# Three loads instead of one ahead of the barrier on entry, in a softmax kernel that is bound by its transfers

## The chip, the cores and the metric

The kernel runs on one core of one Trainium2 chip. The metric is the device time of one execution in microseconds (us); medians of several runs are given. A profile of one execution goes with each kernel. The engines that matter here: VectorE (DVE in the profile), ScalarE (ACT), GpSimd (POOL), SyncE (SP, which issues the loads), and the 16 DMA engines that carry out all loads and stores.

## The reference

```python
x = np.random.randn(16, 1024, 512).astype(np.float32)      # 33.55 MB in, 33.55 MB out

def reference(x):
    x_max = np.max(x, axis=-1, keepdims=True)
    exp_x = np.exp(x - x_max)
    return (exp_x / np.sum(exp_x, axis=-1, keepdims=True)).astype(np.float32)
```

## The kernel before

The 16,384 rows are cut into ten chunks; R is the number of rows that each of the 128 partitions gets. The first chunks are small, so that work can start early. All chunks live in one buffer of SBUF (the on-chip memory) of 96 rows per partition; the last two use places that earlier chunks have left.

```python
CHUNKS = [
    (3, 0), (5, 3), (8, 8), (16, 16), (16, 32), (16, 48), (16, 64), (16, 80), (16, 0), (16, 16),
]                                        # (rows R, place in SBUF)
...
EARLY = 8                                # loads issued at the start
AFTER_STORE = {2: [8], 3: [9]}
GROUP = 8
...
STORE_ROWS = {3: 8, 4: 8, 5: 8}          # chunks not named here are stored whole
ON_ACT = ()                              # loads issued by ScalarE instead of SP
AT_HEAD = {mybir.EngineType.SP: 1}
```

The program begins with a barrier of all engines (line 164 in the profiles). This function takes the first loads of SP out of the body and puts them ahead of SP's part of that barrier:

```python
def loads_at_the_head(nc):
    main, body = nc.main_func.blocks[0], nc.main_func.blocks[1]
    for engine, count in AT_HEAD.items():
        loads = [ ... the engine's first `count` DMA copies in body ... ]
        barrier = ... the engine's first InstDrain in main ...
        for load in loads:
            body.instructions.remove(load)
        main.instructions[barrier:barrier] = loads
```

The schedule, shortened:

```python
    for k, (R, _) in enumerate(CHUNKS):
        m = max(1, round(R / GROUP))     # groups of about 8 rows
        ...
    for k in range(EARLY):
        load(k)                          # nc.sync.dma_start
    for g, (k, a, _, _) in enumerate(groups):
        ...
        rowmax(g)     # VectorE, line 101: reduce_max, negated
        exps(g)       # ScalarE, line 109: exp with bias, and the row's sum
        scale(...)    # VectorE, lines 121, 123: reciprocal, multiply; then the store, issued by ScalarE, line 129
```

## Time and profile before

| | before |
|---|---|
| time, median of the 3 first runs | 161.57 us (161.53 to 161.69) |
| span of the profiled execution | 159.7 us |
| VectorE busy | 123.9 us (78%) |
| ScalarE busy | 93.3 us (58%) |
| bytes moved | 67.1 MB, mean 420 GB/s |

VectorE is at 78% over the span, but at 98% from 60 to 140 us, and idle at both ends.

### The profile page before, as it was taken

How to read it: one execution, taken by the hardware profiler on the slowest of the kernel's cores; microseconds unless marked ns; L12 is line 12 of the kernel's file. 1: busy time of each engine (PE TensorE's matmuls, PEld its weight loads, DVE VectorE, ACT ScalarE, POOL GpSimd, SP SyncE). 2: the span in 40 equal slices, each digit the busy share in tenths (PEclk: the TensorE clock that was granted, in tenths of full speed). 3: DMA queues.
4: the chain of work that ended last, by engine and by line, in shares of the span. 5: the costliest groups of instructions: out<-in, count | busy, mean ns of one | idle time of the engine just before them, and what ended most of it. 6: DMA issues, size and time to landing. Idle time of an engine off the chain costs nothing.

```text
span 159.7 us, 521 instructions
## 1 busy us (share of the span) xinstructions
DVE 123.9 (78%) x162; ACT 93.3 (58%) x257; POOL 0.2 (0%) x4
## 2 busy tenths in 40 slices
DVE  0481870799699999999999999999999999762000
ACT  0718129208994959595868677686859595930000
POOL 0000000000000000000000000000000000000000
DMA  7999999899999999999999999999999999999993
GB/s 269 433 464 411 389 447 446 383 412 466 402 441 431 460 435 396 439 418 468 427 414 439 414 484 427 396 447 402 435 439 476 418 402 468 443 402 468 427 410 164
DMA packets 3315, 67.13 MB, mean 420 GB/s; under 512 B 368, under 2 KB 368, under 8 KB 624
## 3 DMA queue, kind: packets, MB, share of 16 engines
q1 hardware_dynamic: 1440, 33.56, 49.5%
q10 hardware_dynamic: 1872, 33.56, 48.9%
q14 instruction: 3, 0.02, 0.0%
HBM read 33.55 MB, written 33.55 MB: 420 GB/s over the span
## 4 chain that ended last, share of the span: by engine, by line
DVE 70%; ACT 14%; issue 3%; DMA 3%; DVEq 0%; ACTq 0%
DVE shift L101 38%; DVE held L123 30%; ACT held L109 14%; DMA held<-in_x_dram 3%; DVE recip L121 2%; DVEq L175 0%; ACTq L109 0%
## 5 line engine op out<-in xcount | busy, mean ns | idle before, releaser
L109 ACT ACTIVATE held<-held,shift 128x512 f32<-128x512 f32 x128 | 90.5, 709 | 43.4 <-DVE shift L101 33.2
L101 DVE TENSOR_REDUCE shift<-held 128x8 f32<-128x4096 f32 (+2 forms) x17 | 70.6, 4161 | 4.5 <-DMA held<-in_x_dram 4.5
L123 DVE TENSOR_SCALAR held<-held,recip 128x512 f32<-128x512 f32 x128 | 52.2, 481 | 0.6
L109 ACT ACTIVATION_READ_ACCUMULATOR held<-held,shift 128x1 f32 x128 | 24.0, 187 | 0.0
L121 DVE RECIPROCAL recip<-sums 128x8 f32<-128x8 f32 (+2 forms) x17 | 3.3, 193 | 15.8 <-ACT held L109 15.8
L109 ACT ACT_TABLE_LOAD x1 | 1.3, 1283 | 4.5 <-DMA held<-in_x_dram 4.5
L164 POOL MEMSET const-bfloat16-1.0<- 128x1 bf16 x1 | 0.1, 102 | 0.0
L164 POOL MEMSET const-uint8-127<- 128x1 uint8 x1 | 0.1, 102 | 0.0
L164 POOL MEMSET const-float32-1.0<- 128x1 f32 x1 | 0.1, 99 | 0.0
L164 POOL MEMSET const-float32-0.0<- 128x1 f32 x1 | 0.1, 98 | 0.2 <-issue 0.2
## 6 DMA issues: line engine op xcount, KB each, us to landing
held<-in_x_dram SPq DMA_DIRECT2D x7, 4096.0 KB, 41.8
out_dram<-held ACTq DMA_DIRECT2D x4, 4096.0 KB, 21.0
out_dram<-held ACTq DMA_DIRECT2D x7, 2048.0 KB, 35.5
held<-in_x_dram SPq DMA_DIRECT2D x1, 2048.0 KB, 11.3
held<-in_x_dram SPq DMA_DIRECT2D x1, 1280.0 KB, 6.7
out_dram<-held ACTq DMA_DIRECT2D x1, 1280.0 KB, 20.0
held<-in_x_dram SPq DMA_DIRECT2D x1, 768.0 KB, 4.5
out_dram<-held ACTq DMA_DIRECT2D x1, 768.0 KB, 15.7
```

The costliest lines, as they stand in the source:

```text
L101: nc.vector.reduce_max(out=shift[g], in_=place[k][:, a:b, :], axis=AX, negate=True)
L109: nc.scalar.activation(out=place[k][:, r, :], in_=place[k][:, r, :], func=EXP, bias=shift[g][:, r - a : r - a + 1], scale=1.0, accum_out=s ...
L121: nc.vector.reciprocal(out=recip, in_=sums[g])
L123: nc.vector.tensor_scalar_mul(out=place[k][:, r, :], in0=place[k][:, r, :], scalar1=recip[:, r - a : r - a + 1],)
L164: nc = _bacc.Bacc("TRN2", target_bir_lowering=False, num_devices=1)
```

## The change

The intent: when the first load's bytes are through, the next loads should already stand in the queue. Two lines change.

```diff
-AT_HEAD = {mybir.EngineType.SP: 1}
+AT_HEAD = {mybir.EngineType.SP: 3}
...
-        m = max(1, round(R / GROUP))
+        m = -(-R // GROUP)
```

## The prediction

> **What bounds the kernel now.** I read the page's picture of the 40 slices first, to see which resource is full and where it isn't.
>
> ```profile
> DVE  0481870799699999999999999999999999762000
> ACT  0718129208994959595868677686859595930000
> DMA  7999999899999999999999999999999999999993
> GB/s 269 433 464 411 389 447 446 383 412 466 402 441 431 460 435 396 439 418 468 427 414 439 414 484 427 396 447 402 435 439 476 418 402 468 443 402 468 427 410 164
> ```
>
> A slice is 159.7 / 40 = 4.0 us. The DMA row is full everywhere but in the first and the last slice. VectorE (DVE) is full in the middle but idle in the last three or four slices, while the DMA engines still work. So the bytes set the end: 33.55 MB in and 33.55 MB out. To see how full "full" is, and what happens in the first microseconds, I asked for busy time in chosen windows; the last three columns are granted clock, DMA share and GB/s.
>
> ```profile
> 0.00:1.00 1.00, 0.00 (x0) 0.00 (x0) 0.20 (x4) 1.00 0.00 0
> 1.00:2.00 1.00, 0.00 (x0) 0.00 (x0) 0.00 (x0) 1.00 0.98 289
> 2.00:3.00 1.00, 0.00 (x0) 0.00 (x0) 0.00 (x0) 1.00 0.94 362
> 3.00:4.00 1.00, 0.00 (x0) 0.00 (x0) 0.00 (x0) 1.00 1.07 432
> 8.00:60.00 52.00, 40.27 (x49) 28.84 (x81) 0.00 (x0) 1.00 1.01 429
> 60.00:140.00 80.00, 78.41 (x104) 60.21 (x169) 0.00 (x0) 1.00 1.00 432
> 140.00:157.00 17.00, 3.46 (x9) 1.21 (x4) 0.00 (x0) 1.00 1.00 432
> ```
>
> At 432 GB/s the 67.1 MB alone need 155.3 us of the 159.7. Only 4.4 us of the span are anything else. At the head: 1.0 us with no byte moved, then two microseconds below the later rate, which lose (432 - 289) / 432 + (432 - 362) / 432 = 0.33 + 0.16 = 0.5 us. The other 2.9 us are the tail and the small shortfalls between. The change can only touch the head, so this 1.5 us (0.9% of the time) is all that it could ever win.
>
> Next, when SP issues its loads (columns: start, duration, engine and line; I put four narrow windows of the timeline under each other), and when the barrier on entry comes.
>
> ```profile
> 0.00 0.37 SPq L96 DMA_DIRECT2D held<-in_x_dram  x1
> ...
> 0.78 0.33 SPq L96 DMA_DIRECT2D held<-in_x_dram  x1
> ...
> 1.16 0.42 SPq L96 DMA_DIRECT2D held<-in_x_dram  x1
> ...
> 1.63 0.59 SPq L96 DMA_DIRECT2D held<-in_x_dram  x1
> ```
>
> ```profile
> L164 SPq DRAIN  x1: 131/131/131, 0.4 to 0.4; - x1
> L164 SPq EVENT_SEMAPHORE  x1: 17/17/17, 0.7 to 0.7; - x1
> ```
>
> The first load is issued at 0.00, then SP drains, goes through the barrier at 0.7, and issues the second load at 0.78, the third at 1.16, the fourth at 1.63. Between the end of the first issue (0.37) and the start of the second (0.78) lie 0.41 us, where two issues that follow each other in the body are only some 0.05 us apart (0.78 + 0.33 = 1.11 to 1.16). So the barrier costs SP about 0.36 us.
>
> Last, who uses these loads, and when (timeline of VectorE and of ScalarE's last store; then the page's issues with the time to landing in the last column):
>
> ```profile
> 4.48 1.75 DVE L101 TENSOR_REDUCE shift<-held 128x3 f32<-128x1536 f32 x1 [4.48 <-DMA held<-in_x_dram]
> ...
> 9.93 2.81 DVE L101 TENSOR_REDUCE shift<-held 128x5 f32<-128x2560 f32 x1
> ...
> 18.65 4.41 DVE L101 TENSOR_REDUCE shift<-held 128x8 f32<-128x4096 f32 x1
> ...
> 144.77 0.34 ACTq L129 DMA_DIRECT2D out_dram<-held  x1
> ```
>
> ```profile
> held<-in_x_dram SPq DMA_DIRECT2D x1, 2048.0 KB, 11.3
> held<-in_x_dram SPq DMA_DIRECT2D x1, 1280.0 KB, 6.7
> ...
> held<-in_x_dram SPq DMA_DIRECT2D x1, 768.0 KB, 4.5
> ```
>
> The first load lands at 4.46 and releases VectorE. The second lands at 0.78 + 6.7 = 7.5 and is read at 9.93, with 2.4 us to spare; the third lands at 1.16 + 11.3 = 12.5 and is read at 18.65, with 6.2 us to spare. Neither of the two loads that move is waited for. The chain of waits goes through VectorE, but its last instruction releases a 2 MB store at 144.77, which alone would need 2.1 MB / 432 GB/s = 4.9 us and so could be over by 150; the DMA runs to 158.5 (last packet in the trace) because earlier stores stand before it. VectorE therefore has some 8 us in hand at the end.
>
> **What the Trainium skill says.** Four places of the page "DMA: Bandwidth & Descriptors" bear on this. (1) "Queues, rings and completion order": on each DMA engine a queue's descriptors are consumed in ring order. The trace agrees: the packet records of the second load (10,240 bytes each) begin at 3.12 us, as those of the first (6,144 bytes) run out on one engine after another, though it was issued at 0.78. (2) "Latency and other measured facts": the first byte of a transfer issued by SP or ScalarE comes after about 600 ns. Here the first packet starts at 1.02 us, 0.65 us after the end of its issue (0.37). (3) "Specifications": a ceiling of 435 GB/s for the 16 engines; the trace moves 432 GB/s from 60 to 157 us, so there is no faster state for the change to reach. (4) "Issuing engines are not separate DMA queues": starting transfers concurrently on several engines saves only the sequencer's issue time. The change also saves issue time only, though on one engine; what that is worth is worked out below.
>
> **The change part by part.** *The grouping line.* m = max(1, round(R / 8)) becomes the ceiling of R / 8. For the sizes used, 3, 5, 8 and 16, the old line gives 1, 1, 1, 2 and the new one 1, 1, 1, 2. The order of instructions agrees: VectorE's 52 rows, ScalarE's 29 and the others are identical, and only SP's order differs. Cost: 0.
>
> *The loads at the head.* Nothing is removed or added. Two DMA issues of SP move from behind the barrier to before it. First the second load: its issue would begin at 0.37 + 0.05 = 0.42 instead of 0.78, the third at 0.42 + 0.33 + 0.05 = 0.80 instead of 1.16, each 0.36 us earlier. For that to be worth something, an engine must have run dry before the second load came. With the 1.02 us from start of issue to first packet, the second load was ready to move at 0.78 + 1.02 = 1.80, and the first engine became free for it at 3.12. It stood in the queue for 1.3 us already; now it stands there from 1.44, for 1.7 us. Gain on the path: 0.
>
> *The barrier.* SP arrives at it after three issues instead of one: 0.80 + 0.42 = 1.22 instead of 0.37, so 0.85 us later, and the others pass it at about 0.7 + 0.85 = 1.55. VectorE and ScalarE have nothing to do until the first load lands at 4.46, so 2.9 us of slack remain. ScalarE's table load also began only after that landing, at 4.53, and lay beside the first reduction. Loss on the path: 0.
>
> *The fourth load on.* SP's sum up to the fourth issue is the same three issues and one barrier in another order, so it still starts near 1.6, and its packets begin only at 11.25 us in the trace. The sixth load waits for the first one's landing (4.47) and the two last wait for stores; none of these moves. Effect: 0.
>
> Sum: 0 gained at the head, 0 lost, DMA bytes and rate unchanged. Predicted time: the time before, 161.6 us rounded.
>
> **The rivals.** *An idle DMA is filled, so it is faster.* For it: the first slice shows 269 GB/s and there is a 0.41 us hole in SP. Against it: in the windows 1:2 and 2:3 the engines are 98% and 94% busy already; the rate is low because the packets take long (the first ones 0.3 to 0.7 us, later ones of the same size 0.23 us), not because none are queued. If earlier queueing did lift these two microseconds to the full rate, 0.5 us would go: 161.1. The first 1.0 us stays, as the first load's issue doesn't move.
>
> *The first load now shares the engines with the next two, and lands late.* If the three were served in turn and not in ring order, the first would land after some 3 x 0.79 = 2.4 MB instead of 0.79 MB: 1.6 MB / 432 GB/s = 3.7 us later. VectorE would end near 148.4, still before the stores are through, and the DMA would have loads to move meanwhile. The time would grow by a few tenths, at most about 1 us: 161.6 to 162.6. Ring order in the trace speaks against it.
>
> *The later barrier becomes the wait.* It would need to pass 4.46, 3.8 us later than before, where two issues cost 0.85. If it did by x us, VectorE's 8 us in hand would take it up first. Time: 161.6.
>
> *The order of loads and stores falls differently.* Any shift of a tenth of a microsecond may change how packets of the two queues alternate. The slices vary from 383 to 484 GB/s, but even out over windows of 50 us and more (429, 432). I allow 0.3 us either way for it.
>
> **Range and chances.** The three runs before lie within 0.16 us (161.53 to 161.69). Beside this come the 0.3 us of the last rival, 0.5 us at best from a better start, and at worst about half a microsecond of a late first load. I take 161.55, with 161.0 to 162.1. Faster by over 2% would need 3.2 us, twice the whole 1.5 us at the head: 0.01. Slower by over 2% would need a stall that no view suggests: 0.01. Within 2%: 0.98.
>
> **What would show each step right or wrong.** In the profile after: SP issues at about 0.00, 0.42 and 0.80, the fourth near 1.6; the barrier at about 1.55. The first reduction still starts at 4.4 to 4.6; if it starts past 5, the sharing rival holds. The window from 1 to 4 us keeps about 360 GB/s (289, 362 and 432 before); if it rises above 400, the idle-DMA rival holds. The second load's issue to landing grows by about 0.36, from 6.7 to 7.1, as it waits longer in the queue and lands at the same 7.5; the third's from 11.3 to 11.7. The window from 60 to 140 us stays at 430 GB/s. The prediction is wrong if the span leaves 159.1 to 160.3, or if the mean rate in the middle moves by more than 1%.

## The result, and the profile after

| | before | after |
|---|---|---|
| time, median (range) of 4 runs | 161.56 (161.53 to 161.69) | 161.61 us (161.46 to 161.69) |
| ratio, with its 95% interval | | 1.0001 (0.9983 to 1.0018) |
| span of the profiled execution | 159.7 | 159.7 us |

Ratios here and below are the mean time of one kernel's fast runs over that of the other's of the same rounds, so they are not quite the ratio of the medians quoted. The outputs are correct. The time is the same.

The picture of the 40 slices after:

```profile
DVE  0481870799699999999999999999999999762000
ACT  0718029208994959595867777686859594930000
DMA  7999999899999999999999999999999999999993
GB/s 274 436 464 424 389 425 464 375 404 466 410 445 443 456 415 412 439 415 480 419 415 427 410 501 410 412 435 402 447 439 476 402 419 484 402 419 460 427 410 164
```

The DMA row is the same digit for digit, the first slice included. The chosen windows after (granted clock, DMA share and GB/s are the last three columns):

```profile
0.00:1.00 1.00, 0.00 (x0) 0.00 (x0) 0.20 (x4) 1.00 0.00 0
1.00:2.00 1.00, 0.00 (x0) 0.00 (x0) 0.00 (x0) 1.00 0.98 264
2.00:3.00 1.00, 0.00 (x0) 0.00 (x0) 0.00 (x0) 1.00 0.93 387
3.00:4.00 1.00, 0.00 (x0) 0.00 (x0) 0.00 (x0) 1.00 1.09 442
60.00:140.00 80.00, 78.36 (x104) 60.18 (x169) 0.00 (x0) 1.00 1.00 432
```

The first microsecond still moves nothing, the next three move 264 + 387 + 442 = 1093 KB against 289 + 362 + 432 = 1083 KB before, and the middle runs at the same 432 GB/s. SP's issues (four narrow windows of the timeline) and its part of the barrier (the line's own view) after:

```profile
0.00 0.37 SPq L96 DMA_DIRECT2D held<-in_x_dram  x1
...
0.42 0.42 SPq L96 DMA_DIRECT2D held<-in_x_dram  x1
...
0.89 0.43 SPq L96 DMA_DIRECT2D held<-in_x_dram  x1
...
1.73 0.51 SPq L96 DMA_DIRECT2D held<-in_x_dram  x1
```

```profile
L164 SPq DRAIN  x1: 125/125/125, 1.4 to 1.4; - x1
L164 SPq EVENT_SEMAPHORE  x1: 17/17/17, 1.6 to 1.6; - x1
```

So the edit did what it was meant to do: the second load is issued 0.36 us earlier, the third 0.27 us, and the barrier falls 0.9 us later. Its users, and the last store, after (timeline), and the three issues with the time to landing in the last column:

```profile
4.40 1.75 DVE L101 TENSOR_REDUCE shift<-held 128x3 f32<-128x1536 f32 x1 [4.40 <-DMA held<-in_x_dram]
...
9.85 2.81 DVE L101 TENSOR_REDUCE shift<-held 128x5 f32<-128x2560 f32 x1
...
144.71 0.34 ACTq L129 DMA_DIRECT2D out_dram<-held  x1
```

```profile
held<-in_x_dram SPq DMA_DIRECT2D x1, 2048.0 KB, 11.4
held<-in_x_dram SPq DMA_DIRECT2D x1, 1280.0 KB, 7.0
...
held<-in_x_dram SPq DMA_DIRECT2D x1, 768.0 KB, 4.4
```

The second load now takes 7.0 us to land where it took 6.7, and so lands at 0.42 + 7.0 = 7.4 us against 7.5. Almost all of what SP gained is spent waiting in the queue. The first load lands at 4.4 us as before, and VectorE starts with it.

### The profile page after: what moved, and what is told of

Its sections match the earlier page's. It is cut to its first block, busy times and chain, and to the rows that moved or that the text cites. A ratio compares the mean times of both kernels' runs of the same rounds, so it can differ in the third digit from the quotient of the medians.

```text
span 159.7 us, 521 instructions
## 1 busy us (share of the span) xinstructions
DVE 123.9 (78%) x162; ACT 93.3 (58%) x257; POOL 0.2 (0%) x4
## 4 chain that ended last, share of the span: by engine, by line
DVE 71%; ACT 14%; issue 3%; DMA 3%; DVEq 0%; ACTq 0%
DVE shift L101 38%; DVE held L123 30%; ACT held L109 14%; DMA held<-in_x_dram 3%; DVE recip L121 2%; DVEq L175 0%; ACTq L109 0%
```

## The experiments

The main theory: the DMA engines have work from the first packet to the last, so only the moment of the first packet and the bytes count; a load that is queued before it is needed gains nothing by being queued earlier. Rivals: VectorE's chain sets the end; SP's hole between the loads costs time; several loads at once hurt the first. All runs below give correct outputs unless it is said.

A yardstick serves for several of them: the bytes moved in the first 8 us, from the windows view. A deficit divided by 432 GB/s is what the end should lose if the transfers set it. The kernel before moves 8 x 350 = 2800 KB, the changed one 8 x 354 = 2832 KB.

**No load at the head.**

```diff
-AT_HEAD = {mybir.EngineType.SP: 1}
+AT_HEAD = {}
```

> No load is ahead of the barrier; all ten follow it. Main theory (the DMA engines are full from the first packet to the end, so only the issue of the first load counts, and how many follow it at the head does not): the first issue moves from before the barrier to behind it, some 0.6 to 0.7 us later on the clock of the other engines, so the time grows by about 0.6 us to 162.2 us (162.0 to 162.4). Rival (VectorE's chain or the middle sets the end and has several us in hand): no change, 161.6 us. A rate in the middle of 432 GB/s in either case.

Measured: 162.32 us (162.26 to 162.50), ratio 1.0036 (1.0019 to 1.0054). The first load is issued at 0.73 us, and 8 x 322 = 2576 KB are moved in 8 us: a deficit of 224 KB, or 0.5 us. The mean of the runs grew by 0.0036 x 161.6 = 0.6 us. So moving the *first* load does pay, most of its 0.73 us (0.3 to 0.9 us by the interval); the head of the program is on the path.

**Five loads at the head.**

```diff
-AT_HEAD = {mybir.EngineType.SP: 3}
+AT_HEAD = {mybir.EngineType.SP: 5}
```

> Five loads ahead of the barrier. SP reaches it after five issues, and the others pass it near 2.7 us (0.7 before, 1.65 with three). Main theory: all wait for the first load's landing at 4.4 to 4.5 us anyway, so no change: 161.6 us (161.4 to 161.8). Rival (more issues ahead of the barrier cost or win a little each, and with three they cancelled): a drift of 0.2 us or more away from the kernel before, in either direction.

Measured: 161.61 us (161.54 to 161.83), ratio 0.9992 (0.9975 to 1.0010). SP passes the barrier at 3.1 us instead of 0.7, later than the 2.7 expected because one issue took 0.94 us, and nothing comes of it. One, three and five loads give the same time: only the first of them counts, and the barrier has room up to the first landing.

**Seven and eight loads at the head: the barrier made to be the wait.**

```diff
-AT_HEAD = {mybir.EngineType.SP: 3}
+AT_HEAD = {mybir.EngineType.SP: 7}        # and 8
```

> Seven loads ahead of the barrier; the sixth and seventh wait for the landing of the first and the second load, so SP reaches the barrier near 7.8 us, and VectorE starts near 7.9 instead of 4.4: a shift of 3.4 to 3.5 us of its whole chain. By the prediction on record (8 us in hand at the end): no change, 161.6 us. By the packet records, read again after the result: the last store is 4 MB and not 2 MB, it is issued at 144.77 and its packets begin at 147.65 on the first DMA engine and at 148.85 on the last, so it was ready (issue + 1.02 = 145.8) only 1.9 to 3.0 us early; the shift is then 0.4 to 1.6 us too long: 162.0 to 163.2 us.

> Eight loads ahead of the barrier; the eighth waits for the third load's landing at 12.4 us, so VectorE starts near 12.9 instead of 4.4: a shift of 8.4 us. By the prediction on record (8 us in hand): 162.0 us at most. By the packet records (1.9 to 3.0 us in hand): 5.4 to 6.5 us slower, 167.0 to 168.1 us, if no wait inside VectorE's chain takes up a part.

Measured: with seven 162.38 us (162.35 to 162.51), ratio 1.0033 (1.0015 to 1.0050); with eight 176.89 us (176.79 to 177.03), ratio 1.0930. Timeline of the run with seven:

```profile
8.46 1.75 DVE L101 TENSOR_REDUCE shift<-held 128x3 f32<-128x1536 f32 x1 [8.46 <-PEq L164]
...
148.76 0.34 ACTq L129 DMA_DIRECT2D out_dram<-held  x1
```

And of the run with eight:

```profile
22.75 1.75 DVE L101 TENSOR_REDUCE shift<-held 128x3 f32<-128x1536 f32 x1 [22.75 <-PEq L164]
...
163.04 0.34 ACTq L129 DMA_DIRECT2D out_dram<-held  x1
```

VectorE is now released by line 164, the barrier, and no longer by the load. With seven it starts 8.46 - 4.40 = 4.06 us later than in the changed kernel, and the last store is issued 148.76 - 144.71 = 4.05 us later: nothing inside VectorE's chain takes up the shift. In the packet records no packet is in flight at 149.5 us, and the last store's first 16 packets begin at 149.61 to 149.75 us, so the DMA engines had run out of work, and the last packet ends at 159.51 instead of 158.47. Of 4.05 us, 1.04 reached the end, so VectorE had 3.0 us in hand. With eight the shift is 22.75 - 4.40 = 18.35 us and the last packet ends at 173.78, 15.3 us later: again 3.0 us in hand. (These are differences of single profiled runs; by the ratios, which compare with the kernel before in the same rounds, the losses are 0.5 and 15.0 us, and the room 3.5 and 3.3 us. So it is about 3 us.) My expected shift for eight (8.4 us) was wrong, since the eighth load is issued only at 21.98 us, after the fourth load's landing, and not after the third's at 12.4; the sum of shift and room holds all the same. The 8 us of the prediction are refuted.

**Less work for VectorE.** Wrong result on purpose: only the first row of each group is multiplied.

```diff
-        for r in range(a, b):
+        for r in range(a, a + 1):
             nc.vector.tensor_scalar_mul(
```

> The changed kernel, but only the first row of each group is multiplied by the reciprocal (111 of 128 multiplications gone; the result is wrong on purpose, all loads and stores stay). VectorE loses about 111 x 0.41 = 45 us. Main theory (bytes set the end): no change beyond 0.5 us, 161.1 to 162.0 us, with VectorE idle part of the middle. Rival (VectorE's chain sets the end): tens of us faster, or at least the 1.9 us that its last store would come earlier.

Measured: 161.80 us (161.75 to 161.87), ratio 0.9998 (0.9983 to 1.0013). The page of that run:

```profile
DVE 81.1 (51%) x51; ACT 92.5 (58%) x257; POOL 0.2 (0%) x4
```

VectorE loses 123.9 - 81.1 = 42.8 us of work and the time doesn't move. Together with the two runs before: VectorE does not set the end, but it is only about 3 us of delay away from doing so.

**The first two loads in two queues.** The second load goes to ScalarE's head.

```diff
-ON_ACT = ()
+ON_ACT = (1,)
-AT_HEAD = {mybir.EngineType.SP: 3}
+AT_HEAD = {mybir.EngineType.SP: 1, mybir.EngineType.Activation: 1}
```

> The first load at SP's head and the second at ScalarE's head, both before the barrier, so the two stand in different queues of the same DMA engines. Main theory (within one queue the first load is served first; of two queues the engines take turns): the first load lands later than 4.4 us, between 5.0 and 6.4, and the second earlier than 7.5; VectorE starts 0.6 to 2.0 us later, inside the 1.9 to 3.0 us that it has in hand, so the time stays within 0.3 us of 161.6. If the first load lands at 4.4 to 4.6 here as well, taking turns does not show, and ring order is not what protected it in the changed kernel.

Measured: 161.76 us (161.62 to 161.87), ratio 0.9994 (0.9979 to 1.0010). Issues of that run:

```profile
held<-in_x_dram ACTq DMA_DIRECT2D x1, 1280.0 KB, 9.7
...
held<-in_x_dram SPq DMA_DIRECT2D x1, 768.0 KB, 5.8
```

The first load takes 5.8 us instead of 4.4, and VectorE starts at 5.87. The Trainium skill says why ("DMA: Bandwidth & Descriptors", "Queues, rings and completion order"): an engine takes turns between the queue rows that have work. In the changed kernel the three loads stand in one queue and the first lands at 4.4 us, so it is this order that protects it. The 1.5 us that VectorE loses here are inside its 3.0 us, and the time stays. I had expected the second load to land earlier than 7.5 us; it landed at 0.1 + 9.7 = 9.8, because SP's third load now shared with it (93 of its 128 packets start between 5.0 and 9.8 us).

**The second load held back.** The converse of the change, made from the kernel before: the load must wait until an engine has written to its place.

```diff
         for k in range(EARLY):
+            if k == 1:
+                nc.vector.memset(place[1][:, 0:2, :], 0.0)
             load(k)
```

> The kernel before with the second load held back on purpose until VectorE has cleared 2 rows of its place (about 1 us), so it is issued near 1.4 to 2.0 us and not at 0.78. Main theory: ready to move at issue + 1.02 = 2.4 to 3.0 us, still before the first DMA engine runs out of the first load at 3.1 us, so no change: 161.6 us (161.4 to 161.8), and the window from 1 to 4 us keeps some 360 GB/s. Rival (each tenth of a microsecond of SP's hole between the two loads costs time, so closing it should have paid): 0.6 to 1.2 us slower, 162.2 to 162.8 us.

For the long hold the added line is `nc.vector.tensor_copy(out=place[1][:, 0, 0:1], in_=place[0][:, 0, 0:1])`, which waits for the first load.

> The kernel before with the second load held back until the first has landed and VectorE has copied one element of it: issued at 4.6 to 4.7 us, first packet near 5.7. Main theory: the slowest DMA engine ends its part of the first load near 4.1 us and then stands still until 5.7, so every byte behind it comes 1.5 to 2.0 us later: 163.1 to 163.6 us. Rival (VectorE's chain sets the end, DMA has time in hand): the second load lands near 11.5 instead of 7.5 us, 1.5 us after VectorE wants it at 10.0, and the time grows by 0 if VectorE has more than that in hand.

Measured: short hold 163.24 us (163.01 to 163.32), ratio 1.0090 (1.0072 to 1.0108); long hold 164.54 us (164.52 to 164.66), ratio 1.0174 (1.0152 to 1.0195). The long hold confirms the mechanism and shows that I sized it too small. Its windows:

```profile
3.00:4.00 1.00, 0.00 (x0) 0.00 (x0) 0.00 (x0) 1.00 0.39 160
4.00:5.00 1.00, 0.48 (x2) 0.43 (x1) 0.00 (x0) 1.00 0.00 0
5.00:6.00 1.00, 1.00 (x1) 0.86 (x1) 0.00 (x0) 1.00 1.03 164
```

I had counted the stop of the slowest engine, about 1.6 us from 4.1 to 5.7. But at 3.5 us only 3 packets are in flight, so 13 of the 16 engines stand still by then; the mean over all engines is 2.3 us. In addition, from 5 to 6 us they are busy and move only 164 GB/s: the first 16 packets after the stop take 1.03 us on average and up to 1.40, where the median of that size is 0.385, so they lose another 0.6 us. Together that is 2.9 us. The yardstick has 8 x 190 = 1520 KB, a deficit of 1280 KB or 3.0 us; the mean grew by 2.8 us.

The short hold is a miss: issued at 1.99 us, 1.2 us later than before, it should have cost nothing by the prediction's margin of 1.3 us, and it cost 0.0090 x 161.6 = 1.5 us. In its packet records most DMA engines begin the second load by 4.2 us, but two only at 6.4 and 6.6 us, though the last engine had ended its part of the first load at 4.15. (The records name no engine; what they show is 14 packets in flight instead of 16 until 6.3 us.) The end is uneven too: the 16 engines finish between 157.87 and 160.22 us, two of them after 160, against 157.33 to 158.53 before. That these are the same two is likely and not shown.

**A control, and three more doses.** The control clears two rows at the same time, but in the eighth load's place, so that the second load isn't held:

```diff
+            if k == 7:
+                nc.vector.memset(place[7][:, 0:2, :], 0.0)
```

> Control for the short hold: the same clearing of 2 rows by VectorE at the same moment, but in the place of the eighth load, which is issued late in any case; the second load is not held. If the 1.6 us of the short hold came from holding the second load: no change here, 161.6 us (161.4 to 161.8). If they came from VectorE writing while the first load arrives: 163.0 to 163.3 us again.

The other three are the short hold with one element cleared (`place[1][:, 0, 0:1]`), with one row (`place[1][:, 0, :]`), and with two rows cleared by GpSimd (`nc.gpsimd.memset`).

> The second load held until VectorE has cleared one element of its place: issued near 1.15 us instead of 0.78, so held back by as much as the change brings it forward. If the queue's margin is what the prediction says (1.3 us): no change, 161.6 us (161.4 to 161.8). If the margin is smaller and is used up step by step, so that the short hold's 1.2 us of delay cost 1.6 us: some 0.3 to 0.5 us slower, 161.9 to 162.1 us.

> The second load held until VectorE has cleared one row of its place: issued near 1.5 us instead of 0.78, 0.75 us later than before. By the prediction's margin of 1.3 us: no change, 161.6 us (161.4 to 161.8). If there is a threshold that depends on the last DMA engine to be fed rather than the first, between 1.5 and 2.0 us: no change here either, against 1.6 us at 1.99. If the loss grows in step with the delay: about 1.0 us slower, 162.6 us.

> The short hold again, but GpSimd clears the 2 rows and VectorE does nothing extra: the second load issued between 1.9 and 2.8 us. If holding the load is the cause, whoever holds it: 1.0 to 2.2 us slower, 162.6 to 163.8 us, and some DMA engines begin the second load late again. If VectorE's write was: 161.6 us. It also tells whether two engines standing still until 6.4 us was an accident of one trace or comes back.

Measured, with the other runs in order of the second load's issue:

| run | second load issued at, us | KB in the first 8 us | median (range), us | ratio (95%) |
|---|---|---|---|---|
| changed kernel | 0.42 | 2832 | 161.61 (161.46 to 161.69) | 1.0001 (0.9983 to 1.0018) |
| control, not held | 0.78 | 2816 | 161.61 (161.54 to 161.67) | 0.9992 (0.9972 to 1.0011) |
| one element | 0.92 | 2408 | 162.49 (162.14 to 163.43) | 1.0057 (1.0026 to 1.0087) |
| one row | 1.46 | 2328 | 162.37 (162.20 to 163.16) | 1.0051 (1.0025 to 1.0076) |
| GpSimd, two rows | 1.75 | 2592 | 163.07 (162.63 to 163.74) | 1.0085 (1.0061 to 1.0109) |
| short hold | 1.99 | 2400 | 163.24 (163.01 to 163.32) | 1.0090 (1.0072 to 1.0108) |
| long hold | 4.71 | 1520 | 164.54 (164.52 to 164.66) | 1.0174 (1.0152 to 1.0195) |

The control clears VectorE's write of blame, and GpSimd's version shows that it does not matter who holds the load. The surprise is the smallest dose. Its second issue, and its windows:

```profile
0.92 0.33 SPq L96 DMA_DIRECT2D held<-in_x_dram  x1
```

```profile
3.00:4.00 1.00, 0.00 (x0) 0.00 (x0) 0.00 (x0) 1.00 0.92 334
5.00:6.00 1.00, 1.00 (x1) 0.92 (x1) 0.00 (x0) 1.00 0.93 276
```

And the window from 3 to 4 us of the run with one row:

```profile
3.00:4.00 1.00, 0.00 (x0) 0.00 (x0) 0.00 (x0) 1.00 1.60 268
```

With one element the issue is only 0.14 us later than before, and the rate falls to 334 and 276 GB/s where the kernel before had 432 and 369. In the packet records 25 of the second load's 128 packets take over 0.5 us (4 before), the longest 1.84 us, and three of the 16 engines have no packet in flight for most of the time from 3.5 to 4.3 us. Of the deficit of 392 KB, or 0.9 us, engines without a packet make up 0.2 us and packets that take longer 0.6. With one row held it is 0.1 and 0.9 of 1.1 us: there 13 packets of the second load take 1.26 to 1.72 us, while the DMA share reads 1.60. So most of this loss is slow packets, which the profile shows as busy. My guess of 1.15 us for its issue was wrong, and so was "no change". The loss doesn't grow in step with the delay either: 0.14 and 0.68 us of delay cost about the same, 0.9 and 0.8 us (intervals 0.4 to 1.4 and 0.4 to 1.2). These are means of a mixture: most runs of both kernels lie near 162.2 or near 163.3 us, the two profiles are of runs near 162.2, and none of the upper ones was traced. It looks like an edge near the issue time of the kernel before, past which the DMA engines no longer go on from one load to the next at full rate.

The yardstick is rough here: GpSimd's deficit of 208 KB is 0.5 us and its cost 1.4, the short hold's 400 KB are 0.9 us and its cost 1.5. It counts the mean of all engines, and in both runs the engines end further apart (1.9 and 2.3 us, against 1.2 before).

What stays open: why an engine that has packets of the first load until 3.1 us or later should stop or slow down because the next load was issued at 0.92 and not at 0.78. And each held version differs from the control in two things, the later issue and a semaphore wait on the load; no run separates them. One more hint, no more than that: of the kernel before's 23 runs in all sets, 6 lie between 161.97 and 162.57 us; of the 14 runs with three or five loads at the head (the changed kernel, the five-load one and the one with less work for VectorE), none is above 161.87. That would fit a kernel that sits at the edge and a change that moves it away. But the control, which issues its loads at the times of before, has none above 161.67 in 6 runs, and the runs are too few.

## Why the prediction was right

The time was inside the range (161.61 in 161.0 to 162.1) and the verdict, the same, was the likely one.

- *Bytes set the end.* Shown: 42.8 us less work for VectorE changed nothing, and a deficit of bytes at the head came back at the end (0.5 us against 0.6 measured with no load at the head, 3.0 against 2.8 for the long hold; with the short holds it explains only part, 0.9 of 1.5 and 0.5 of 1.4).
- *The grouping line costs 0.* The orders of instructions of VectorE and ScalarE are identical in the two traces, as the prediction says; both kernels execute 521 instructions.
- *The second load waits in the queue instead of at the barrier: gain 0.* Right in its outcome: it landed at 7.4 instead of 7.5 us, and the window from 1 to 4 us kept its rate. But the step's margin, "It stood in the queue for 1.3 us already", failed: held back on purpose, a load issued 0.14 us later cost 0.9 us, and one issued 1.2 us later cost 1.5 us. I took the start of the first packet of one load, added it to the issue of the next, and compared with the moment when the first engine is free. What the packet records of the held versions show instead is that some engines stop between the loads, and that packets of the second load take up to 1.84 us where 0.385 is usual, well inside that margin; why stays open. The change brought the load forward, so the error did no harm. That was luck: by these runs (medians of 162.4 to 162.5 us for 0.14 and 0.68 us of delay, though with a semaphore wait as well) a change of the same size the other way would have left the range.
- *The later barrier costs 0.* Right: 0.9 us later with three, 2.4 us later with five, no effect; with seven it became the wait.
- *The fourth load on.* Issued at 1.73 instead of 1.63 us and the third at 0.89 instead of the 0.80 foretold, because the second and third issue took 0.42 and 0.43 us where I put 0.33 for the second. No consequence. The list of waits was incomplete: beside the sixth, the seventh and eighth load wait for landings too (issued at 7.51 and 24.31 us before).
- *The rivals.* The gain of 0.5 us from a fuller start did not come: 1093 KB against 1083 KB by 4 us. Late landing of the first load did not come either, and the two-queue run shows that ring order prevents it. For that rival I had claimed that even 3.7 us would cost only a few tenths, from "VectorE therefore has some 8 us in hand at the end". That step was wrong: the last store is 4 MB and not 2 MB. The page listed four stores of 4096 KB, and only chunks 3 to 5 are cut by STORE_ROWS. With 4.2 MB / 432 GB/s = 9.7 us and about 1.0 us to the first packet, the store issued at 144.77 needs until 155.5, which is 3.0 us before 158.5. The room measured is 3.0 us as well. By my estimate a delay of 3.7 us would have cost 0.7.

## What to carry to other kernels

In this kernel, where the transfers never pause, issue time ahead of the first packet is on the path and issue time behind it is hidden: one load at the head was worth 0.6 us, the next two nothing. Ask of each transfer whether the queue had run dry before it, but don't trust a margin that is worked out from the first packet of the first engine; hold the load back by a little and look. Before claiming room on an engine off the path, work out the size of the last transfer that it releases, for that is what stands between its end and the program's.

## What the Trainium skill lacked or had wrong

- "DMA: Bandwidth & Descriptors" has the delay to the first byte (600 ns; 0.65 us here), but no page says how long before a queue runs dry the next transfer must be issued. Here a load held back to 0.92 instead of 0.78 us, with engines busy until 3.1 us and later, cost 0.9 us (the semaphore wait that held it may have a part in it).
- The same page doesn't say that a DMA engine restarts slowly. After a stop of 2.3 us on average, the first 16 packets of 10,240 bytes took 1.03 us on average against a median of 0.385, and 2.8 us were lost in all.
- The same page, "Specifications", gives an HBM limit of about 358 GB/s per core, half of what two cores share; that a core alone gets more is said only further down the page. From 4 to 8 us, with loads alone in flight (the first store is issued at 10.04 us), this one-core program moves 430 GB/s before the change, near the 435 GB/s that the section gives as the fabric's ceiling. So the page is not wrong here, but its table alone would mislead.
